# A two-matrix MLP in split fp32: which operand streams, how wide, and where the residual is added

## The chip, the cores and the metric

One core of a Trainium2 chip runs one program. The metric is the device time of one execution in microseconds (us); lower is better. The profile comes from one execution of its own, so its numbers are compared with that execution's time, and the median of the runs stands beside it. The engines are named as in the profile: PE is TensorE (matmuls), PEld its weight loads, DVE is VectorE, ACT is ScalarE, POOL is GpSimd, SP is SyncE, whose queue issues most DMAs.

## The reference

A decoder block on 256 tokens with a model width of 2048, in fp32. Two token mixers run ahead of the part that matters here, which is the end of the layer and the last normalization:

```python
h = x + gt1 * ((sig(gA) * y_A + sig(gB) * y_B) @ w_out)
u = rmsnorm(h, g_mlp) * (1 + sc2) + sh2
h = h + gt2 * (relu(u @ w_up) ** 2 @ w_down)      # w_up 2048 x 8192, w_down 8192 x 2048
out = rmsnorm(h, g_final)
```

`gt2` (like `sc2` and `sh2`) is a row of 2048 values, one sixth of `silu(c) @ w_ada + b_ada`.

## The kernel before

**Split fp32.** A product of two fp32 matrices is computed with three faster matmuls. Each operand is split into a rounded part `hi` (type fp32r) and a remainder `lo`; the product is hi x hi + hi x lo + lo x hi. For weights, `Unit.prep` makes `hi` with a ScalarE copy (helper `copy`, line 117) and `Unit.prep_lo` makes `lo` with a VectorE subtraction (helper `tt`, line 120). Both work on a raw tile of 128 x 1024 weights that the SP queue has loaded (line 210). There are 7 raw buffers, and 3 each of hi and lo.

**Units.** All work is a list of units, one raw tile each. `run_units` goes through the list: it issues the loads up to 7 units ahead, makes `hi` of unit i, issues the matmuls of unit i-2 (`SPLIT = 2`), then makes `lo` of unit i, then runs what was deferred to this index (`defer(n, fn)` runs `fn` n units later), then the steps of background generators that are due. Each engine works through its own instructions in the order in which they are issued there. A unit that only feeds VectorE (`gemm=False`, the adaLN products) has no hi or lo; `weave` spreads such units among others.

**A pass.** `gemm_pass` computes 1024 output columns. Weights are the loaded operand in blocks of 128x128, and the activations, in channel order (channels on the partitions, 256 tokens in the free dimension), stream as 256 columns. For each of 8 column blocks j, the unit issues three matmuls (lines 315, 317, 318). Two blocks share one PSUM bank, and the four banks A0 to A3 hold a pass. In the last unit of a pass, `finish(b, ps)` is called as soon as bank b is complete, and the next pass starts again with A0. `joint` is the number of units at the end of a pass whose matmuls are held and then issued block by block, so that the banks are completed one after the other.

**The MLP.** The first matrix (`up_units`) is 8 passes of 16 units over the normalized activations in region RU; `finish` is a ReLU out of PSUM into region RX (line 1415), and the square follows one unit later (line 1416). Among these units are woven 32 adaLN units, which sum the products of `w_ada` rows with `cond` for the two halves of `gt2` on VectorE (line 129). At the end of each half `fin1` sums over the partitions with matmuls (line 965) and `fin2` turns the result into columns with four transposes. The second matrix (`down_units`) is 2 passes of 64 units; `xprep` splits the hidden activations on the way (hi and lo of 128x256 per unit). `finish` there adds `gt2` times the result to the residual `hs["h"]`, which is in channel order, scales by `g_final`, squares, and `turn` transposes into token order with four PE transposes per bank (line 1466). The last batch also sums the squares over the channels with matmuls of one column (line 1359), and `last` scales by the reciprocal root and issues eight stores on the SP and ACT queues (line 1492).

**Another product of the same kernel.** `vs_units` computes the value projection the other way round: activations are the loaded operand, and 512 weight columns stream (lines 897 to 899).

Of the kernel before, what the change touches and what calls it, by code (L numbers as in the profile page):

```python
# [36 lines left out]
J_PROJ, J_GLU, J_OUT, J_UP, J_DOWN = 1, 1, (1, 2), 1, (1, 2)  # L37
# [44 lines left out]
def block_kernel(ctx, tc, cst_in, x, c, w_ada, b_ada, g_mix, w_in, w_ck2, pe_ck,  # L82
# [78 lines left out]
    small = cp.tile([128, 8], FT, name="small")  # L161

# [166 lines left out]

    BA = ["A0", "A1", "A2", "A3"]  # L330
# [139 lines left out]
    def rstd(o, ssum, t):  # L470

        A.activation(out=t, in_=ssum, func=AF.Sqrt)
# [511 lines left out]

    def ada2_pe_units(vec, quarter):
# [399 lines left out]
    def u2_start(row):  # L1385
        r = region("RU", 8192)
# [13 lines left out]
    class U2View:  # L1400
        def __init__(self, key):
            self.key = key

        def __getitem__(self, i):
            return u2[self.key][i]

    def up_units():
        res = []
        for g in range(8):
            def finish(b, ps, g=g):  # L1410
                if "h" not in h1:
                    h1["h"] = region("RX", 16384).rearrange("p (k t) -> p k t", k=64)
                ct = g * 8 + 2 * b
                o = h1["h"][:, ct:ct + 2, :].rearrange("p k t -> p (k t)")
                A.activation(out=o, in_=ps, func=AF.Relu)
                defer(1, lambda: A.activation(out=o, in_=o, func=AF.Square))
            res += gemm_pass(w_up[0], 1024 * g, list(range(16)), 1024, True, True, (U2View("h"), U2View("l")), BA, finish, joint=J_UP)
        return res

    fin = {}  # L1420

    def down_units():
        def slot(i):
# [6 lines left out]
        for g in range(2):  # L1430
            made = {}
# [8 lines left out]
            def finish(b, ps, g=g):  # L1440
                if "o" not in fin:
                    fin["u"] = region("RU", 8192)
                    fin["o"] = fin["u"][:, 0:4096].rearrange("p (t n) -> p t n", t=2)
                    fin["acc"] = fin["u"][:, 4096:4608]
                    fin["sq"] = fin["u"][:, 4608:6656]
                    fin["t"] = region("RB1", 4096)
                ct = g * 8 + 2 * b
                h = hs["h"][:, ct:ct + 2, :]
                for j in range(2):
                    stt(h[:, j, :], ps[:, 256 * j:256 * j + 256], gt2_c[:, ct + j:ct + j + 1], h[:, j, :],  # L1450
                        OP.mult, OP.add)
                hv = h.rearrange("p k t -> p (k t)")
                acc = fin["acc"]
                t = fin["t"][:, 512 * b:512 * b + 512]
                for j in range(2):
                    if g == 0 or j == 0:
                        A.activation(out=t[:, 256 * j:256 * j + 256], in_=h[:, j, :], func=AF.Copy,
                                     scale=gfin_c[:, ct + j:ct + j + 1])
                    else:
                        ts(t[:, 256 * j:256 * j + 256], h[:, j, :], gfin_c[:, ct + j:ct + j + 1], OP.mult)  # L1460

                def turn():
                    pb = bank(("T0", "T3")[b % 2])
                    for tok in range(2):
                        for j in range(2):
                            PE.transpose(pb[:, tok * 256 + j * 128:tok * 256 + j * 128 + 128],
                                         t[:, 256 * j + 128 * tok:256 * j + 128 * tok + 128], ident)
# [150 lines left out]
```

## Time and profile before

| | |
|---|---|
| median of 3 runs | 1780.44 us (1776.47 to 1782.63) |
| time of the profiled execution | 1776.92 us |
| its span | 1775.1 us |
| mean granted TensorE clock | 0.989 |
| PE busy | 1718.9 us, 97% of the span, 15710 matmuls |
| PEld busy | 1620.6 us, 91%, 15710 weight loads |
| DVE busy | 1108.5 us, 62% |
| ACT busy | 856.3 us, 48% |
| DMA moved | 406.26 MB, 229 GB/s on average |
| loads of the two matrices | 128 each, 512 KB each |

How to read it: the duration of a matmul in the trace is from its start to its modelled end, and matmuls overlap, so the distance between starts is what one costs; a group's busy time counts overlaps once. "Idle before" is the time in which an engine had nothing running ahead of an instruction, with what released it. A line number can be that of a helper that many places call.

### The profile page before, as it was taken

How to read it: one execution, taken by the hardware profiler on the slowest of the kernel's cores; microseconds unless marked ns; L12 is line 12 of the kernel's file. 1: busy time of each engine (PE TensorE's matmuls, PEld its weight loads, DVE VectorE, ACT ScalarE, POOL GpSimd, SP SyncE). 2: the span in 40 equal slices, each digit the busy share in tenths (PEclk: the TensorE clock that was granted, in tenths of full speed). 3: DMA queues.
4: the chain of work that ended last, by engine and by line, in shares of the span. 5: the costliest groups of instructions: out<-in, count | busy, mean ns of one | idle time of the engine just before them, and what ended most of it. 6: DMA issues, size and time to landing. Idle time of an engine off the chain costs nothing.

```text
span 1775.1 us, 37647 instructions
## 1 busy us (share of the span) xinstructions
PE 1718.9 (97%) x15710; PEld 1620.6 (91%) x15710; DVE 1108.5 (62%) x2032; ACT 856.3 (48%) x1379; POOL 29.4 (2%) x51
## 2 busy tenths in 40 slices
PE   6999999999999999999999999999999999999997
PEld 4788898789999988888899999999999999999997
DVE  4868468347888966666656575555555555565554
ACT  3433443754333477655544454444444544464444
POOL 1000000300000000000000000000000000000000
PEclk8999999999999999999999999999999999999998
DMA  9988756858888867876667567777777565556662
GB/s 349 327 275 315 260 180 206 267 160 296 274 274 283 254 211 243 296 244 211 214 198 262 176 219 235 235 227 224 240 234 227 179 183 184 181 176 184 184 181 81
DMA packets 121802, 406.26 MB, mean 229 GB/s; under 512 B 13904, under 2 KB 18480, under 8 KB 120864
## 3 DMA queue, kind: packets, MB, share of 16 engines
q1 hardware_dynamic: 114480, 385.49, 67.1%
q10 hardware_dynamic: 5408, 9.75, 1.5%
q0 software_dynamic: 1744, 8.62, 1.4%
q8 instruction: 123, 2.02, 0.4%
q14 instruction: 47, 0.39, 0.1%
HBM read 384.84 MB, written 16.88 MB: 226 GB/s over the span
## 4 chain that ended last, share of the span: by engine, by line
PE 87%; DVE 5%; ACT 4%; DMA 2%; issue 1%; ACTq 0%; SPq 0%; DVEq 0%
PE A L315 25%; PE A L317 24%; PE A L318 24%; PE T L998 2%; DVE lo L120 2%; PE T L343 2%; ACT hi L117 1%; ACT RX L117 1%; DMA raw<-in_l_ada_dram 1%; PE T L809 1%; PE A L897 1%; DMA raw<-in_l_vals_dram 1%; PE A L899 1%; PE A L898 1%; PE T L737 0%
## 5 line engine op out<-in xcount | busy, mean ns | idle before, releaser
L120 DVE TENSOR_TENSOR lo<-raw,hi 128x1024 fp32r<-128x1024 f32 (+1 forms) x497 | 607.0, 1223 | 507.8 <-ACT hi L117 504.0
L117 ACT ACTIVATE hi<-raw 128x1024 fp32r<-128x1024 f32 (+1 forms) x497 | 523.1, 1055 | 580.5 <-PE A L317 539.0
L315 PE MATMUL A<-RU,hi 128*128 128x256 f32 x2560 | 740.2, 289 | 3.3 <-ACT hi L117 1.5
L318 PE MATMUL A<-RU,lo 128*128 128x256 f32 x2560 | 728.0, 284 | 1.5 <-DVE lo L120 1.5
L317 PE MATMUL A<-RU,hi 128*128 128x256 f32 x2560 | 727.8, 284 | 0.0
L315 PEld LDWEIGHTS A<-RU,hi 128*128 128x128 f32 x2560 | 494.3, 193 | 27.7 <-issue 20.9
L318 PEld LDWEIGHTS A<-RU,lo 128*128 128x128 f32 x2560 | 494.4, 193 | 2.0 <-DVE lo L120 1.9
L317 PEld LDWEIGHTS A<-RU,hi 128*128 128x128 f32 x2560 | 494.7, 193 | 0.3 <-DVE RU L129 0.2
L315 PE MATMUL A<-RB,hi 128*128 128x256 f32 x1280 | 363.9, 284 | 1.4 <-ACT RB L117 1.2
L317 PE MATMUL A<-RB,hi 128*128 128x256 f32 x1280 | 362.6, 283 | 0.2
L318 PE MATMUL A<-RB,lo 128*128 128x256 f32 x1280 | 362.2, 283 | 0.0
L315 PEld LDWEIGHTS A<-RB,hi 128*128 128x128 f32 x1280 | 245.7, 192 | 3.4 <-ACT RB L117 1.6
L317 PEld LDWEIGHTS A<-RB,hi 128*128 128x128 f32 x1280 | 245.7, 192 | 0.6 <-DVE RB L129 0.5
L318 PEld LDWEIGHTS A<-RB,lo 128*128 128x128 f32 x1280 | 245.6, 192 | 0.0
L117 ACT ACTIVATE RB<-RX 128x256 fp32r<-128x256 f32 x160 | 64.3, 403 | 27.4 <-DVE RX L129 27.4
L120 DVE TENSOR_TENSOR RX<-A,RX 128x512 f32<-128x512 f32 x60 | 40.4, 687 | 30.2 <-PE A L318 29.2
L129 DVE SCALAR_TENSOR_TENSOR s<-raw,cond,s 128x1024 f32<-128x1024 f32 x45 | 57.6, 1279 | 0.1
L117 ACT ACTIVATE RX<-T 128x256 f32<-128x256 f32 (+2 forms) x81 | 39.8, 638 | 35.8 <-PE T L1204 26.6
L120 DVE TENSOR_TENSOR RB<-RX,RB 128x256 fp32r<-128x256 f32 x128 | 53.4, 418 | 1.6 <-ACT RB L117 1.6
L343 PE MATMUL T<-raw,cond 128*32 128x256 f32 x512 | 40.8, 413 | 10.0 <-DMA raw<-in_l_ada_dram 10.0
L998 PE MATMUL T<-raw,cond 128*32 128x128 f32 x1280 | 43.2, 276 | 2.0 <-ACT RX L117 2.0
L998 PEld LDWEIGHTS T<-raw,cond 128*32 128x32 f32 x1280 | 32.5, 109 | 8.4 <-ACT RX L117 4.2
(237 smaller groups left out, 1248.1 us busy)
## 6 DMA issues: line engine op xcount, KB each, us to landing
raw<-in_l_ada_dram SPq DMA_DIRECT2D x144, 512.0 KB, 4.9
raw<-in_w_in_dram SPq DMA_DIRECT2D x144, 512.0 KB, 4.6
raw<-in_w_up_dram SPq DMA_DIRECT2D x128, 512.0 KB, 4.2
raw<-in_w_down_dram SPq DMA_DIRECT2D x128, 512.0 KB, 4.5
raw<-in_w_ada_dram SPq DMA_DIRECT2D x48, 512.0 KB, 4.1
raw<-in_w_glu_dram SPq DMA_DIRECT2D x32, 512.0 KB, 5.1
raw<-in_w_out_dram SPq DMA_DIRECT2D x32, 512.0 KB, 5.8
raw<-in_l_keys_dram SPq DMA_DIRECT2D x16, 512.0 KB, 4.4
```

Source lines behind the costliest of these rows:

```text
L117: A.activation(out=out, in_=in_, func=AF.Copy, scale=scale)
L120: V.tensor_tensor(out=out, in0=a, in1=b, op=op)
L129: V.scalar_tensor_tensor(out=out, in0=a, scalar=s, in1=b, op0=op0, op1=op1)
L315: PE.matmul(out=o, lhsT=w.hi[:, at], rhs=xh, start=first and j % 2 == 0, stop=False, skip_group_check=True)
L317: PE.matmul(out=o, lhsT=w.hi[:, at], rhs=xl, start=False, stop=False, skip_group_check=True)
L318: PE.matmul(out=o, lhsT=w.lo[:, at], rhs=xh, start=False, stop=last, skip_group_check=True)
L343: PE.matmul(out=ps[q:q + 32, :], lhsT=cond[:, t0 + t:t0 + t + 1].to_broadcast([128, 32]), rhs=r[:, t, :], start=t0 == 0, stop=t0 == 12, ti ...
L809: PE.matmul(out=ps[h][:, (w * 2 + r_) * 128:(w * 2 + r_) * 128 + 128], lhsT=bl[c4 // 2][64 * h:64 * h + 64, (gw + w) % 16, r_, :], rhs=stk ...
L897: PE.matmul(out=o, lhsT=xh, rhs=u.hi[:, at], start=kt == 0, stop=False)
L898: PE.matmul(out=o, lhsT=xl, rhs=u.hi[:, at], start=False, stop=False)
L899: PE.matmul(out=o, lhsT=xh, rhs=lo[:, at], start=False, stop=kt == 15)
L998: PE.matmul(out=ps[q:q + 32, 0:128], lhsT=cond[:, kt:kt + 1].to_broadcast([128, 32]), rhs=r[:, kt % 8, :], start=kt < 4, stop=kt >= 12, ti ...
```

## The change

* First matrix: pass 0 (1024 columns) stays as it was, now with its own `finish` called `first`. The remaining 7168 columns become 14 passes of 512 columns in `wide_pass`. A unit holds two k blocks of 128 rows with 512 columns each, loaded as two runs of 512 values per partition. For each of 4 column blocks and both k blocks there are two matmuls: `hi` against 512 columns, which are the hi and the lo activations side by side (a view with two pieces of 256), and `lo` against the 256 hi activations. A bank now holds one column block, with the lo activations' share in its upper half. `finish` copies that half on ScalarE, adds the lower half on VectorE, and one unit later VectorE computes max(v, 0) * v.
* Second matrix: the activations become the loaded operand (two token halves t), and 512 weight columns stream (two halves s_ of the 1024). There are 12 matmuls per unit, and the result is in token order. In pass 1 the last 3 units are held, where it was 2.
* `gt2` is made as a row on all partitions instead of columns: `row_units` replaces `ada2_units(3, ...)`, with four matmuls against a full block of ones, and the bias row and `g_final` are broadcast by two DMAs on POOL's queue.
* The residual is transposed into token order by a background generator, `h_tokens`, in eight steps during pass 0 of the second matrix.
* The finish works in token order: products with the rows, sums of squares through `accum_out`, the mean and root per token half, and eight stores, all on the SP queue. For columns 0 to 1023 the product with `g_final` is deferred work in pass 1.

```diff
-J_PROJ, J_GLU, J_OUT, J_UP, J_DOWN = 1, 1, (1, 2), 1, (1, 2)
+J_PROJ, J_GLU, J_OUT, J_UP, J_DOWN = 1, 1, (1, 2), 1, (1, 3)
...
+    def wide_pass(src, col0, pairs, finish):
+        made, res = {}, []
+
+        def run(u, k0):
+            if k0 == 0:
+                made["b"] = [bank(t) for t in BA]
+            for j in range(4):
+                o = made["b"][j]
+                for t in range(2):
+                    xp = pairs(k0 + t)
+                    at = slice(512 * t + 128 * j, 512 * t + 128 * j + 128)
+                    PE.matmul(out=o, lhsT=u.hi[:, at], rhs=xp, start=k0 + t == 0, stop=False, skip_group_check=True)
+                    PE.matmul(out=o[:, 0:256], lhsT=u.lo[:, at], rhs=xp[:, 0], start=False, stop=k0 + t == 15,
+                              skip_group_check=True)
+                if k0 == 14:
+                    finish(j, o)
+
+        for k0 in range(0, 16, 2):
+            v = src[k0 * 128:(k0 + 2) * 128, col0:col0 + 512].rearrange("(k p) n -> p k n", p=128)
+            res.append(Unit([(lambda r: r.rearrange("p (k n) -> p k n", k=2), v)], lambda u, k=k0: run(u, k)))
+        return res
...
+    def row_units():
+        def place():
+            r = region("RB1", 4096)
+            rows["g"], rows["f"] = r[:, 0:2048], r[:, 2048:4096]
+            nc.gpsimd.dma_start(out=rows["g"], in_=b_ada[:, A_GT2:A_GT2 + D].to_broadcast([128, D]))
+            nc.gpsimd.dma_start(out=rows["f"], in_=g_final.rearrange("(o n) -> o n", o=1).to_broadcast([128, D]))
...
+            def fin_(i):
+                ps = bank("T3")
+                PE.matmul(out=ps, lhsT=ones, rhs=hold["a"][:, 512 * i:512 * i + 512], start=True, stop=True)
+                o = rows["g"][:, 1024 * half + 512 * i:1024 * half + 512 * i + 512]
+                tt(o, ps, o, OP.add)
+                if i == 0:
+                    defer(FIN_GAP, lambda: fin_(1))
...
     def up_units():
...
+        def pairs(kt):
+            return fr(u2["r"]).rearrange("p (s k t) -> p k s t", s=2, k=16)[:, kt]
...
+        res += gemm_pass(w_up[0], 0, list(range(16)), 1024, True, True, (Part("h"), Part("l")), BA, first, joint=J_UP)
+        for g in range(2, 16):
             def finish(b, ps, g=g):
...
+                if b % 2 == 0:
+                    h1["st"] = stage()
+                st = h1["st"][:, 256 * (b % 2):256 * (b % 2) + 256]
+                copy(st, ps[:, 256:512])
+                tt(st, ps[:, 0:256], st, OP.add)
+                if b % 2:
+                    st = h1["st"]
+                    ct = g * 4 + b - 1
+                    o = h1["h"][:, ct:ct + 2, :].rearrange("p k t -> p (k t)")
+                    defer(1, lambda: stt(o, st, 0.0, st, OP.max, OP.mult))
+            res += wide_pass(w_up[0], 512 * g, pairs, finish)
...
+    def h_tokens():
+
+        fin["u"] = region("RU", 8192)
+        fin["h"] = fin["u"][:, 0:4096].rearrange("p (t n) -> p t n", t=2)
+        fin["m"] = fin["u"][:, 4096:6144]
+        for i in range(8):
+            t, q = i // 4, i % 4
+            ps = bank(("T0", "T3")[i % 2])
+            for j in range(4):
+                PE.transpose(ps[:, 128 * j:128 * j + 128], hs["h"][:, 4 * q + j, 128 * t:128 * t + 128], ident)
+            copy(fin["h"][:, t, 512 * q:512 * q + 512], ps)
+            yield
...
+            def finish(t, c, ps):
+                h = fin["h"][:, t, 512 * c:512 * c + 512]
+                cs = slice(512 * c, 512 * c + 512)
+                m = fin["m"][:, 512 * (2 * t + c % 2):512 * (2 * t + c % 2) + 512]
+                if c < 2:
...
+                    defer(10 + 2 * t + c, lambda: tt(h, h, rows["f"][:, cs], OP.mult))
+                    return
+                tt(m, ps, rows["g"][:, cs], OP.mult)
+                tt(h, m, h, OP.add)
+                A.activation(out=m, in_=h, func=AF.Square, accum_out=ssq[:, 4 * t + c:4 * t + c + 1])
+                if (t, c) == (1, 2):
+                    mean(0)
+                if (t, c) == (1, 3):
+                    roots(0)
+                    mean(1)
+                    store(0, 3)
+                    roots(1)
+                    store(0, 0)
+                    store(1, 3)
...
+            def store(t, q):
+                r_ = small[:, 2 + t:3 + t]
+                v = fin["h"][:, t, 512 * q:512 * q + 512]
+                if q >= 2:
+                    stt(v, v, r_, rows["f"][:, 512 * q:512 * q + 512], OP.mult, OP.mult)
                 else:
...
+                    A.activation(out=v, in_=v, func=AF.Copy, scale=r_)
+                nc.sync.dma_start(out=out[0, t * 128:t * 128 + 128, 512 * q:512 * q + 512], in_=v)
+
+            def run(u, kt, g=g, held=held, acc=acc, finish=finish):
+                if kt == 0:
+                    acc["b"] = [bank(t) for t in BA]
+                held.append((u, kt))
+                if kt != 63 and 64 - kt <= J_DOWN[g]:
+                    return
+                for t in range(2):
+                    for s_ in range(2):
+                        o = acc["b"][2 * t + s_]
+                        at_ = slice(512 * s_, 512 * s_ + 512)
+                        for w, k in held:
+                            xh, xl = (x_[:, 128 * t:128 * t + 128] for x_ in w.xs)
+                            PE.matmul(out=o, lhsT=xh, rhs=w.hi[:, at_], start=k == 0, stop=False)
+                            PE.matmul(out=o, lhsT=xl, rhs=w.hi[:, at_], start=False, stop=False)
+                            PE.matmul(out=o, lhsT=xh, rhs=w.lo[:, at_], start=False, stop=k == 63)
+                        if kt == 63:
+                            finish(t, 2 * g + s_, o)
+                held.clear()
...
-        units += up[:UP_WAIT] + weave(up[UP_WAIT:], [u for h in range(2) for u in ada2_units(3, h, "T3")])
+        units += up[:UP_WAIT] + weave(up[UP_WAIT:], row_units())
...
+            dict(name="ht", gen=h_tokens(), start=marks["down"] + 6, end=marks["down"] + 46, total=8),
```

## Rows read from the trace of the kernel before

**Rows 1.** Page, part 4: the chain that ended last, share of the span by engine.
```profile
PE 87%; DVE 5%; ACT 4%; DMA 2%; issue 1%; ACTq 0%; SPq 0%; DVEq 0%
```

**Rows 2.** Windows in the first and second matrix: busy us (instructions), PEclk, DMA share, GB/s.
```profile
1020.00:1380.00 360.00, 360.00 (x2985) 357.66 (x2985) 200.07 (x184) 166.35 (x195) 0.00 (x0) 1.00 0.72 229
1400.00:1752.00 352.00, 352.00 (x2937) 352.00 (x2936) 195.03 (x255) 172.94 (x260) 0.00 (x0) 1.00 0.58 176
```

**Rows 3.** TensorE's waits, 985 to 1765 us: total us, times, longest us.
```profile
PE A L315 <- ACT RU L386: 1.5, 1, 1.5
PE T L1378 <- DVE small L129: 1.3, 1, 1.3
```

**Rows 4.** Timeline, second matrix: start us, us, engine, line, op, shapes, [idle before].
```profile
1700.64 0.28 PE L315 MATMUL A<-RB,hi 128*128 128x256 f32 x1
...
1700.72 1.06 ACT L117 ACTIVATE hi<-raw 128x1024 fp32r<-128x1024 f32 x1 [1.52 <-PE A L317]
...
1701.81 1.22 DVE L120 TENSOR_TENSOR lo<-raw,hi 128x1024 fp32r<-128x1024 f32 x1 [1.32 <-ACT hi L117]
...
1703.52 0.28 PE L315 MATMUL A<-RB,hi 128*128 128x256 f32 x1
```

**Rows 5.** Timeline, TensorE, value projection: matmuls of 512 columns.
```profile
293.58 0.39 PE L898 MATMUL A<-hi,RU 128*128 128x512 f32 x1
...
298.57 0.39 PE L899 MATMUL A<-lo,RU 128*128 128x512 f32 x1
...
316.51 0.40 PE L898 MATMUL A<-hi,RU 128*128 128x512 f32 x1
...
318.83 0.39 PE L899 MATMUL A<-lo,RU 128*128 128x512 f32 x1
```

**Rows 6.** Timeline of the end; then the DMA share in 40 slices, 1766 to 1775.1 us.
```profile
1761.89 0.28 PE L318 MATMUL A<-RB,lo 128*128 128x256 f32 x1
...
1762.21 0.88 DVE L129 SCALAR_TENSOR_TENSOR RS<-A,ada,RS 128x256 f32<-128x256 f32 x2
...
1763.14 0.61 ACT L1351 ACTIVATE RU<-RS 128x512 f32<-128x512 f32 x1
...
1766.95 2.41 SPq L1492 DMA_DIRECT2D out_dram<-RU  x4
...
DMA  0000000189999999999999999999999930000000
```

**Rows 7.** Lines by shape, VectorE (busy us, mean ns); one ScalarE line of the timeline.
```profile
L120 DVE TENSOR_TENSOR lo<-raw,hi 128x1024 fp32r<-128x1024 f32 x496 | 606.1, 1224 | 502.0 <-ACT hi L117 498.2 <-DMA d_v<-st 2.5 <-DMA raw<-in_l_ada_dram 1.1
...
L120 DVE TENSOR_TENSOR RB<-RX,RB 128x256 fp32r<-128x256 f32 x128 | 53.4, 418 | 1.6 <-ACT RB L117 1.6
L120 DVE TENSOR_TENSOR RX<-A,RX 128x512 f32<-128x512 f32 x60 | 40.4, 687 | 30.2 <-PE A L318 29.2
...
1014.79 0.38 ACT L117 ACTIVATE rbc<-T 128x256 f32<-128x256 f32 x1 [1.77 <-PE T L1378]
```

**Rows 8.** Timeline, TensorE: sums over partitions, attention scores, and four transposes.
```profile
760.40 0.62 PE L1153 MATMUL T<-RX 128*128 128x272 f32 x2
760.86 0.62 PE L1154 MATMUL T<-RX 128*128 128x272 f32 x2
...
1371.62 0.28 PE L318 MATMUL A<-RU,lo 128*128 128x256 f32 x1
...
1373.03 0.28 PE L317 MATMUL A<-RU,hi 128*128 128x256 f32 x1
...
1577.83 0.28 PE L318 MATMUL A<-RB,lo 128*128 128x256 f32 x1
...
1578.51 0.28 PE L317 MATMUL A<-RB,hi 128*128 128x256 f32 x1
```

**Rows 9.** DMA, 840 to 868 us: queue, packets, MB, share; issues, KB, us to landing.
```profile
q1 hardware_dynamic: 2352, 5.77, 61.7%
...
raw<-in_w_glu_dram SPq DMA_DIRECT2D x7, 512.0 KB, 4.5
```

More of the change, by code (lines that the diff above doesn't have):

```diff
@@ L161, in block_kernel @@
     small = cp.tile([128, 8], FT, name="small")
+    ssq = cp.tile([128, 8], FT, name="ssq")
     ru = region("RU", 8192)
@@ L468, in keep_x, with rstd @@
         yield
-    def rstd(o, ssum, t):
-        A.activation(out=t, in_=ssum, func=AF.Sqrt)
+    def rstd(o, ssum, t, rooted=False):
+        if not rooted:
+            A.activation(out=t, in_=ssum, func=AF.Sqrt)
         V.reciprocal(out=o, in_=t)
@@ new lines, in up_units, with __init__, __getitem__, first @@
+        class Part:
+            def __init__(self, key):
+                self.key = key
+            def __getitem__(self, i):
+                return u2[self.key][i]
+        def first(b, ps):
+            if "h" not in h1:
+                h1["h"] = region("RX", 16384).rearrange("p (k t) -> p k t", k=64)
+            o = h1["h"][:, 2 * b:2 * b + 2, :].rearrange("p k t -> p (k t)")
+            A.activation(out=o, in_=ps, func=AF.Relu)
+            defer(1, lambda: A.activation(out=o, in_=o, func=AF.Square))
@@ L1430, in down_units @@
         for g in range(2):
-            made = {}
+            made, held, acc = {}, [], {}
             def xprep(kt, made=made):
@@ L1438, in xprep @@
                 return made[kt]
[L1440 to L1458, printed above, removed]
-                    else:
[L1460 to L1467, printed above, removed]
-                    o = fin["o"][:, :, ct * 128:ct * 128 + 256]
-                    copy(o, pb.rearrange("p (t n) -> p t n", t=2))
-                if g == 0:
-                    defer(1, lambda: sumsq(hv, acc, ct == 0))
-                    defer(1 + b, turn)
-                else:
-                    squares(b, hv, acc, fin["sq"][:, 512 * b:512 * b + 512], fin.pop("turn", None))
-                    fin["turn"] = turn
-                    if b == 3:
-                        turn()
-                        last()
@@ L1496, in weave @@
+            for kt in range(64):
+                u_ = Unit([(lambda r: r, w_down[0, kt * 128:(kt + 1) * 128, 1024 * g:1024 * g + 1024])],
+                          lambda u, k=kt, run=run: run(u, k), xprep=lambda k=kt, xprep=xprep: xprep(k))
+                u_.joint = J_DOWN[g] > 1 and kt == 63
+                res.append(u_)
+        return res
     def weave(main, extra, tail=6, head=0):
```

66 lines of the change are left out of this document (39 added, 27 removed).

## The prediction, made blind

> **What bounds the kernel now.** I read the chain of waits first: 87% of the chain that ended last is TensorE work, 5% VectorE, 4% ScalarE [rows 1]. Then the stretches of the two matrices that the change touches. In the first matrix's 360 us and in 352 us of the second's, TensorE is busy for the whole stretch at a granted clock of 1.00 (2.4 GHz), VectorE for 200 and 195 us, ScalarE for 166 and 173 us, and the DMA engines are at 0.72 and 0.58 [rows 2]. Last, what TensorE waited for from the end of the output projection to the end of the second matrix: two waits, 2.8 us together, both ahead of the first matrix [rows 3]. So in both matrices the time is the number of matmuls times the spacing of their starts; the reported 0.28 us of one overlaps the next ones and is no price. The spacing: the first matmul of one weight part starts at 1700.64, that of the next at 1703.52, with 24 matmuls of 256 columns in each, so 120.0 ns each [rows 4]. 256 columns at 2.4 GHz are 106.7 ns; 13.3 ns are something else, paid once per 256 columns.
>
> The same kernel shows matmuls of 512 columns, with the activations as the loaded operand and the weight columns streaming, which is what the second matrix will have. In the longest stretch without a pause, 22 starts lie between 293.58 and 298.57: 226.8 ns each [rows 5]. 512 columns are 213.3 ns, so the excess is 13.5 ns, the same as at 256 columns: it goes with the matmul, not with the column. In shorter stretches, ten after a stop, it is 232 ns (316.51 to 318.83) [rows 5].
>
> **The change, step by step.** *First matrix, 14 of 16 parts.* Before, a 128x128 block of weights meets three matmuls of 256 columns (hi with both activation parts, lo with one). After, it meets one of 512 and one of 256. There are 14 x 8 units x 8 blocks = 896 of each. One pair of 240.0 ns becomes 226.8: 896 x 13.2 ns = **-11.8 us**. No row has a 512-column operand made of two pieces of 256, nor 512 and 256 in turn. The bounds: it costs like two of 256 (240 ns, nothing gained), or the excess of the narrow matmul vanishes behind the wide one (another 896 x 13.3 = 11.9 us gained). I take the fixed excess, since both widths show it.
>
> *Second matrix.* 2 x 64 units had 24 matmuls of 256; they get 12 of 512. 3072 x 120.0 = 368.6 us become 1536 x 226.8 = 348.4: **-20.3 us**. With 232 ns it would be 356.4, so -12.3. I take 226.8 because the stages of the change run without stops, as that stretch did.
>
> The Trainium skill speaks against both: "TensorE: Matmul & The Clock Gate" (section "Back-to-back issue gap") gives a warm gap of columns/2.4 ns plus about 2.5 ns. By it a pair of 256 costs 218.4 and a 512 costs 215.8, the 2432 replacements would give 6.3 us instead of 32.1, and the sum below would be -6.0 us. Rows 4 and 5 disagree with it at both widths, by some 11 ns, in matmuls that each load new weights.
>
> *The new evictions of the first matrix.* They leave TensorE's path if they end in time. A unit lasts 8 x (226.8 + 120.0) = 2.77 us. Counted from the start of a pass's last unit, bank j is complete for its readers at 0.69 x (j + 1) + 0.20 us (a reader starts 0.32 us after the start of the bank's last matmul, 1761.89 to 1762.21 [rows 6], so 0.20 after its slot of 0.12). Then a ScalarE copy of 128x256 out of PSUM, 0.38, and a VectorE sum, 0.42 [rows 7]. Bank 0 is free at 1.7, needed at 2.8; bank 3 is free at 3.8, needed at 4.9. What is queued behind the waiting sum on VectorE is the lo part of the unit two ahead: 3.8 + 1.22 [rows 7] = 5.0, and its first matmul wants it at 2 x 2.77 + 0.23 = 5.8. So 0.75 us of cover, and I cost it at nothing; each us beyond it would cost 14 us (14 passes). Behind the waiting copy on ScalarE is the hi part of the unit three ahead, wanted some 3 us later. VectorE is busy for 200 of 360 us now [rows 2]; 56 sums of 0.42 and 28 squares of 0.69 [rows 7] add 43, which leaves room.
>
> *The gate row.* Before, per half of the last adaLN vector, TensorE gives up 1.17 us for the sums over partitions (the second matmul after 1371.62 starts at 1373.03 instead of 0.24 later) [rows 8] and, I take it, what four transposes cost below, 0.44: 3.2 us for both halves. After, four sums of 512 fp32 columns over a full 128x128 operand. Nearest: 272 fp32 columns take 0.46 us (760.40 to 760.86) [rows 8], so 0.87 for 512, and about 0.1 for the change of shape: 4.0 us. **+0.8 us** (between 0 and 2). The two row broadcasts on POOL's queue have nothing behind them and are wanted only after 16 woven products, some 60 units later.
>
> *The residual in token order.* 32 transposes as before, in eight groups of four. One group costs 0.44 us (second matmul after 1577.83 at 1578.51 instead of 1578.07) [rows 8]. Before, seven groups lie ahead of the last matmul and one behind it; after, all eight lie ahead: **+0.4 us**.
>
> *The last three units in one batch.* Three buffers for hi, so the hi part of the last unit can start only when the fourth unit from the end is done. hi starts 0.08 us after the next unit's first matmul, lo 1.09 us later and takes 1.22 (1700.64, 1700.72, 1701.81) [rows 4]: ready at 2.35 us, wanted by the ninth matmul at 8 x 0.227 = 1.81. With two held units, as before, that wait was covered by one more unit. **+0.5 us**.
>
> *The finish.* Before, the last matmul's slot ends at 1762.01, the first store is issued at 1766.95, and the span ends 8.15 us after that at 1775.1 [rows 6]. The stores keep the DMA engines at nine tenths for 23 of 40 slices of 0.23 us, some 5.3 us for 2.1 MB [rows 6]: they are limited by the transfer, so the first issue counts. After: reader's lag 0.20, product and sum 2 x 0.69 [rows 7], square 0.61 [rows 6], mean, variance and first product about 1.3 by the size of before's small steps (estimate): issue at 3.5 instead of 4.9 us. **-1.4 us** (between +1 and -3).
>
> Sum: -11.8 - 20.3 + 0.8 + 0.4 + 0.5 - 1.4 = -31.8 us. The profiled execution took 1776.9 us (span 1775.1), the median of the runs is 1780.4. I put the difference to the median: **1748.6 us**.
>
> **Rivals.** *A: the wide matmul is dearer.* All 2432 at 232 ns give back 12.6 us: 1761.2. Or the two-piece operand costs 240 in the first matrix: 11.8 back, 1760.4. For it: the only long steady stretch at 226.8 is one, eleven shorter ones are between 229 and 233. Against: those have a stop at their head.
> *B: the narrow matmul's excess hides behind the wide one* in the first matrix: 1748.6 - 11.9 = 1736.7. For it: the next weight load has 227 ns instead of 120. Against: after a wide matmul the excess is still 13.5 [rows 5].
> *C: no change.* The excess goes with columns in such streams, or with weight traffic, and a 512 costs 240 everywhere: 32.1 us go back, 1780.7. The rows of 512 speak against it.
> *D: slower, through the weight loads.* In the 14 wide parts a load reads runs of 2 KB instead of 4 KB. 360 us at 229 GB/s are 82.4 MB [rows 2]; 112 loads of 0.524 MB are 58.7 of these, 0.51 of the share of 0.72. If 2 KB runs cost twice per byte, the share is 1.23, that is 443 us of transfer in a stage in which TensorE needs 348: 83 us more than now, 20 us gained elsewhere, 1843. It decides from 1.49 times the cost per byte. Against: 840 to 868 us, where most of the moved bytes are 2 KB runs of the GLU weight, 5.77 MB take 61.7% of 28 us, 334 GB/s of busy engine, and such a load lands after 4.5 us [rows 9]; the stretch of 4 KB runs has 229/0.72 = 318. So 2 KB runs are no dearer.
>
> **How the numbers follow.** Forecast 0.64 (its own range 1741 to 1756, from the gate row, finish and pace); A 0.18; B 0.08; C 0.05; D 0.03; 0.02 for something unnamed. From 1738 to 1763 the range holds the forecast, A, and the nearer half of B; left out are C, D, the rest of B. Faster by over 0.3% (5.3 us, about what a measurement of this kernel can tell from none): forecast, A, B and half of the unnamed, 0.91. Same: C, 0.05. Slower: D and the other half, 0.04.
>
> **What would show it.** Right: starts 227 ns after a wide and 120 ns after a narrow matmul, 2.77 us per unit in the first matrix and 2.72 in the second; no wait of TensorE at the 14 pass ends; one wait of about 0.5 us for lo in the last batch; the first store about 3.5 us after the last matmul's slot; the two stages some 12 and 20 us shorter, and everything ahead of them unchanged. Wrong: 232 or 240 ns between wide starts; a wait for lo after each pass; waits of the hi copy for a weight load; a DMA share near 1 in the first matrix. If the two stages shrink by under 20 us together, the term of the fixed excess was mis-sized.

## The result, and the profile after

The changed kernel takes 1754.1 us (median of 4 runs, 1750.1 to 1755.8) against 1780.5 us before: ratio 0.9853, 95% interval 0.9832 to 0.9875, 26.4 us less. Forecast were 1748.6 us and 31.8 us less. The direction and most of the size are right; 5 us are missing. The experiments separate two main causes: a pair of matmuls that costs more than forecast, and waits that were not forecast.

The page after: span, busy time by engine, and the chain's shares, which answer to [rows 1].

```profile
span 1754.0 us, 32823 instructions
...
PE 1693.2 (97%) x13246; PEld 1490.6 (85%) x13246; DVE 1150.7 (66%) x2120; ACT 841.7 (48%) x1376; POOL 30.5 (2%) x53
...
PE 86%; DVE 5%; ACT 5%; DMA 2%; issue 1%; ACTq 0%; SPq 0%; DVEq 0%
```

There are 2464 matmuls fewer, and TensorE is still 97% busy and 86% of the chain. PEld fell from 91 to 85%: a wide matmul leaves time in which no weight load runs.

The windows of the kernel before, cut at three points of each trace: the first matmul of the first matrix, the first of the second matrix, and the end of the last matmul's slot. Columns as in [rows 2].

```profile
1016.29:1390.75 374.46, 374.46 (x3088) 371.88 (x3089) 208.55 (x195) 174.50 (x207) 0.00 (x0) 0.99 0.71 225
1390.75:1762.01 371.26, 371.26 (x3098) 371.22 (x3097) 206.35 (x274) 185.16 (x282) 0.00 (x0) 1.00 0.56 171
1762.01:1775.10 13.09, 4.02 (x34) 3.62 (x32) 3.91 (x13) 5.44 (x10) 0.00 (x0) 0.62 0.44 160
```

The same three windows after:

```profile
1019.59:1386.67 367.08, 367.08 (x2185) 323.88 (x2185) 244.53 (x277) 165.31 (x209) 0.00 (x0) 0.99 0.71 229
1386.67:1742.10 355.43, 353.22 (x1570) 290.84 (x1568) 211.14 (x277) 181.47 (x276) 0.00 (x0) 1.00 0.54 178
1742.10:1754.00 11.90, 0.16 (x1) 0.00 (x0) 5.53 (x16) 3.80 (x10) 0.00 (x0) 0.73 0.50 176
```

The first matrix is 7.4 us shorter (374.46 to 367.08), the second 15.8 (371.26 to 355.43), the finish 1.2 (13.09 to 11.90): 24.4 us together. All that lies ahead is the same code, yet the first matmul of the first matrix starts at 1016.3 in one profile and at 1019.6 in the other. So the spans differ by 21.1 us only (1775.1 to 1754.0). In the other profiles shown below that start lies anywhere from 1013.6 to 1020.3 us, whatever the edit, so this is the runs' own spread. That is why the stages are compared here, and the medians for the total. The DMA share in the first matrix is 0.71 in both windows: the loads in runs of 2 KB cost no more, and they land after 4.0 us.

What TensorE waited for after, from 980 to 1760 us, answering to [rows 3]:

```profile
PE A L316 <- ACT RU L411: 1.5, 1, 1.5
PE A L1603 <- DVE lo L120: 1.4, 3, 0.5
PE T L1440 <- DVE small L129: 1.3, 1, 1.3
PE A L1601 <- ACT hi L117: 0.8, 1, 0.8
```

The first and third row are the old ones. There is no wait at the ends of the 14 passes: the new evictions stay under their cover. The other two are in the second matrix: 1.4 us for `lo`, 0.8 us for `hi`. One of the four times is the last batch, as forecast. The other three are not in the prediction.

The new matmuls of the first matrix, an excerpt in the middle of a pass (PE lines, start first):

```profile
1099.95 0.40 PE L344 MATMUL A<-RU,hi 128*128 128x512 f32 x1
1100.19 0.28 PE L345 MATMUL A<-RU,lo 128*128 128x256 f32 x1
1100.31 0.40 PE L344 MATMUL A<-RU,hi 128*128 128x512 f32 x1
...
1101.37 0.40 PE L344 MATMUL A<-RU,hi 128*128 128x512 f32 x1
```

From 1099.95 to 1101.37 are four pairs, so 355 ns here. Over the whole stretch, leaving out the four places where a sum for the gate row comes between, the trace's starts in ns give 235.4 ns from a wide to the narrow one behind it and 116.7 from there to the next wide: 352.1 ns for a pair, where 226.8 + 120.0 = 346.8 was forecast. (The expectations below have 234.7 and 117.3, from starts rounded to 10 ns as the timeline prints them; the sum is the same.) The second matrix, in a stretch without a stop:

```profile
1582.27 0.39 PE L1601 MATMUL A<-hi,RB 128*128 128x512 f32 x1
...
1584.99 0.39 PE L1601 MATMUL A<-hi,RB 128*128 128x512 f32 x1
```

12 matmuls in 2.72 us: 226.7 ns, the forecast.

Where the unforeseen waits are: VectorE, ScalarE and one restarted matmul (of the three between 1586 and 1593 us) early in the second matrix's second pass, with the idle time before each and its releaser.

```profile
1582.76 0.42 DVE L120 TENSOR_TENSOR RB<-RX,RB 128x256 fp32r<-128x256 f32 x1
...
1583.10 0.69 DVE L120 TENSOR_TENSOR RU<-RU,RB 128x512 f32<-128x512 f32 x1
...
1583.82 0.69 DVE L120 TENSOR_TENSOR RU<-RU 128x512 f32<-128x512 f32 x1
...
1584.54 0.63 ACT L1548 ACTIVATE RU<-RU 128x512 f32<-128x512 f32 x1 [2.66 <-DVE RU L120]
...
1585.08 0.19 ACT L1548 ACTIVATION_READ_ACCUMULATOR RU<-RU 128x1 f32 x1
1585.17 1.04 ACT L117 ACTIVATE hi<-raw 128x1024 fp32r<-128x1024 f32 x1
...
1586.25 1.23 DVE L120 TENSOR_TENSOR lo<-raw,hi 128x1024 fp32r<-128x1024 f32 x1 [1.74 <-ACT hi L117]
...
1587.53 0.50 PE L1603 MATMUL A<-lo,RB 128*128 128x512 f32 x1 [0.53 <-DVE lo L120]
...
1587.73 0.68 DVE L120 TENSOR_TENSOR RU<-RU,RB 128x512 f32<-128x512 f32 x1
```

One unit's deferred work is read here in order. On VectorE the product (1583.10) and the sum (1583.82) of the finish come behind the unit's own work. ScalarE's square (1584.54) has been waiting 2.66 us for the sum, with the `hi` copy of the next unit queued behind it; that starts at 1585.17. `lo` follows it at 1586.25, and TensorE gets it at 1587.53. The round goes over two engines one after the other and takes some 4.6 us, where a unit of TensorE takes 2.72. It comes four units in a row.

The end, answering to [rows 6]: the last batch's wait, the last matmul, the last square, the first store.

```profile
1735.62 0.50 PE L1603 MATMUL A<-lo,RB 128*128 128x512 f32 x1 [0.37 <-DVE lo L120]
...
1741.87 0.39 PE L1603 MATMUL A<-lo,RB 128*128 128x512 f32 x1
...
1743.75 0.63 ACT L1555 ACTIVATE RU<-RU 128x512 f32<-128x512 f32 x1 [1.22 <-DVE RU L120]
...
1745.53 0.82 SPq L1587 DMA_DIRECT2D out_dram<-RU  x2
```

The slot of the last matmul ends at 1742.10, and the first store is issued 3.43 us later (3.5 forecast). The span ends 8.5 us after that, where it was 8.15 before.

### The profile page after: what moved, and what is told of

It is laid out like the page before. It is cut to its first block, busy times and chain, and to the rows that moved or that the text cites. A ratio compares the mean times of both kernels' runs of the same rounds, so it can differ in the third digit from the quotient of the medians.

```text
span 1754.0 us, 32823 instructions
## 1 busy us (share of the span) xinstructions
PE 1693.2 (97%) x13246; PEld 1490.6 (85%) x13246; DVE 1150.7 (66%) x2120; ACT 841.7 (48%) x1376; POOL 30.5 (2%) x53
## 4 chain that ended last, share of the span: by engine, by line
PE 86%; DVE 5%; ACT 5%; DMA 2%; issue 1%; ACTq 0%; SPq 0%; DVEq 0%
PE A L316 12%; PE A L344 12%; PE A L318 12%; PE A L319 12%; PE A L1603 6%; PE A L1601 6%; PE A L1602 6%; PE A L345 6%; PE T L1060 2%; DVE lo L120 2%; PE T L368 1%; ACT hi L117 1%; ACT RX L117 1%; DMA raw<-in_l_ada_dram 1%; DMA raw<-in_l_vals_dram 1%
## 5 line engine op out<-in xcount | busy, mean ns | idle before, releaser
L316 PE MATMUL A<-RU,hi 128*128 128x256 f32 x1664 | 486.0, 292 | 3.3 <-ACT RU L411 1.5
L318 PE MATMUL A<-RU,hi 128*128 128x256 f32 x1664 | 474.2, 285 | 0.0
L316 PEld LDWEIGHTS A<-RU,hi 128*128 128x128 f32 x1664 | 322.4, 194 | 26.4 <-issue 20.1
L318 PEld LDWEIGHTS A<-RU,hi 128*128 128x128 f32 x1664 | 322.6, 194 | 0.3 <-DVE RU L129 0.2
L344 PE MATMUL A<-RU,hi 128*128 128x512 f32 x896 | 317.3, 399 | 0.0
L344 PEld LDWEIGHTS A<-RU,hi 128*128 128x128 f32 x896 | 168.2, 188 | 41.7 <-issue 0.7
L1603 PE MATMUL A<-lo,RB 128*128 128x512 f32 x512 | 199.7, 390 | 1.4 <-DVE lo L120 1.4
L1601 PE MATMUL A<-hi,RB 128*128 128x512 f32 x512 | 200.2, 391 | 0.8 <-ACT hi L117 0.8
L1602 PE MATMUL A<-hi,RB 128*128 128x512 f32 x512 | 199.2, 389 | 0.0
L1603 PEld LDWEIGHTS A<-lo,RB 128*128 128x128 f32 x512 | 96.1, 188 | 22.7 <-DVE lo L120 2.7
L1601 PEld LDWEIGHTS A<-hi,RB 128*128 128x128 f32 x512 | 96.1, 188 | 21.0 <-ACT hi L117 1.4
L1602 PEld LDWEIGHTS A<-hi,RB 128*128 128x128 f32 x512 | 96.1, 188 | 19.6
L316 PE MATMUL A<-RB,hi 128*128 128x256 f32 x256 | 73.6, 287 | 1.4 <-ACT RB L117 1.2
L318 PE MATMUL A<-RB,hi 128*128 128x256 f32 x256 | 72.7, 284 | 0.2
L319 PE MATMUL A<-RB,lo 128*128 128x256 f32 x256 | 72.3, 283 | 0.0
```

Of the source, the lines that this page charges most:

```text
L316: PE.matmul(out=o, lhsT=w.hi[:, at], rhs=xh, start=first and j % 2 == 0, stop=False, skip_group_check=True)
L318: PE.matmul(out=o, lhsT=w.hi[:, at], rhs=xl, start=False, stop=False, skip_group_check=True)
L319: PE.matmul(out=o, lhsT=w.lo[:, at], rhs=xh, start=False, stop=last, skip_group_check=True)
L344: PE.matmul(out=o, lhsT=u.hi[:, at], rhs=xp, start=k0 + t == 0, stop=False, skip_group_check=True)
L1601: PE.matmul(out=o, lhsT=xh, rhs=w.hi[:, at_], start=k == 0, stop=False)
L1602: PE.matmul(out=o, lhsT=xl, rhs=w.hi[:, at_], start=False, stop=False)
```

## The experiments

Each is the changed kernel with the edit shown. Stage times are from the traces, cut as above; "the stretch of the wide passes" is from their first matmul to the first of the second matrix, 318.87 us in the changed kernel.

### One run of 512 columns instead of two pieces

```diff
-                    PE.matmul(out=o[:, 0:256], lhsT=u.lo[:, at], rhs=xp[:, 0], start=False, stop=k0 + t == 15,
+                    PE.matmul(out=o[:, 0:256], lhsT=u.lo[:, at], rhs=xp[:, 0:256], start=False, stop=k0 + t == 15,
...
-        u2["h"] = fr(r[:, 0:4096]).rearrange("p (k t) -> p k t", k=16)
-        u2["l"] = fr(r[:, 4096:8192]).rearrange("p (k t) -> p k t", k=16)
+        v = fr(r).rearrange("p (k s t) -> p k s t", k=16, s=2)
+        u2["h"], u2["l"] = v[:, :, 0, :], v[:, :, 1, :]
...
-            return fr(u2["r"]).rearrange("p (s k t) -> p k s t", s=2, k=16)[:, kt]
+            return fr(u2["r"])[:, 512 * kt:512 * kt + 512]
```

> In the changed kernel a wide matmul of the first matrix and the narrow one behind it take 234.7 + 117.3 = 352.1 ns between starts, where 226.8 + 120.0 = 346.8 was predicted; over 896 pairs that is 4.7 us. Here the hi and lo activations of a k block lie side by side, so that the wide operand is one run of 512 columns. Theory P (the two pieces of the operand cost the 5.3 ns): the pair falls to 346.8 ns and the stretch of the 14 wide passes from 318.9 to about 314.1 us. Theory W (a change of width from one matmul to the next costs it): the pair stays at 352 ns and the stretch at 318.9 us.

```profile
1149.63 0.40 PE L344 MATMUL A<-RU,hi 128*128 128x512 f32 x1
...
1151.75 0.40 PE L344 MATMUL A<-RU,hi 128*128 128x512 f32 x1
```

Six pairs lie between these two starts, 353 ns each. Over the whole stretch it is 235.4 + 116.5 = 351.9 ns for a pair, and 318.73 us. The two pieces are not the cause; theory P falls.

### Wide, wide, narrow, narrow

```diff
-                for t in range(2):
-                    xp = pairs(k0 + t)
...
+                for t in range(2):
+                    at = slice(512 * t + 128 * j, 512 * t + 128 * j + 128)
+                    PE.matmul(out=o, lhsT=u.hi[:, at], rhs=pairs(k0 + t), start=k0 + t == 0, stop=False, skip_group_check=True)
+                for t in range(2):
+                    at = slice(512 * t + 128 * j, 512 * t + 128 * j + 128)
+                    PE.matmul(out=o[:, 0:256], lhsT=u.lo[:, at], rhs=pairs(k0 + t)[:, 0], start=False, stop=k0 + t == 15,
+                              skip_group_check=True)
```

> The order within a column block is wide, wide, narrow, narrow instead of wide, narrow, wide, narrow; operands and their number are as in the changed kernel, the wide one still in two pieces. Theory P (two pieces): four starts take 704.2 ns as before, the stretch of the wide passes stays at 318.9 us. Theory W (changes of width): half of the changes are left, so four starts take 693.6 + 5.3 = 698.9 ns and the stretch shrinks by 2.4 us to 316.5.

Its timeline, where equal neighbours are merged into one row (x2):

```profile
1149.69 0.63 PE L343 MATMUL A<-RU,hi 128*128 128x512 f32 x2
1150.15 0.40 PE L346 MATMUL A<-RU,lo 128*128 128x256 f32 x2
1150.38 0.63 PE L343 MATMUL A<-RU,hi 128*128 128x512 f32 x2
...
1152.47 0.62 PE L343 MATMUL A<-RU,hi 128*128 128x512 f32 x2
```

Four groups of wide and narrow lie between 1149.69 and 1152.47: 695 ns each. Over the whole stretch it is 696.7 on average, and the stretch is 315.52 us, 3.35 less than in the changed kernel. The same matmuls on the same operands, in another order: the direction is theory W's, and the gain is larger than its 2.4 us.

### The deferred finish work in every fourth unit

```diff
                         tt(h, m, h, OP.add)
+
+                    def square():
                         A.activation(out=m, in_=h, func=AF.Square, accum_out=ssq[:, 4 * t + c:4 * t + c + 1])
...
-                    defer(4 + 2 * t + c, rest)
-                    defer(10 + 2 * t + c, lambda: tt(h, h, rows["f"][:, cs], OP.mult))
+                    n = 4 + 4 * (2 * t + c)
+                    defer(n, rest)
+                    defer(n + 1, square)
+                    defer(n + 2, lambda: tt(h, h, rows["f"][:, cs], OP.mult))
```

> In the changed kernel TensorE waits three times between 1586 and 1593 us in the second pass of the second matrix, some 2.7 us with the slower restarts. Theory: the deferred work of the finish (four times a VectorE sum and, right behind it, a ScalarE square that waits for it, in four units in a row) holds back the hi copies behind the squares. Here this work falls in every fourth unit, and the square comes one unit after the sum. Expected: no wait there, the second matrix 2.5 to 2.7 us shorter (355.4 to about 352.8 us from its first matmul to the end of its last slot). Rival (the hi copies wait for raw tiles or free buffers at the change of pass, whatever is deferred): the waits stay, 355.4 us.

TensorE's waits in it, over the same 780 us as above:

```profile
PE A L316 <- ACT RU L411: 1.5, 1, 1.5
PE T L1440 <- DVE small L129: 1.3, 1, 1.3
PE A L1607 <- DVE lo L120: 0.4, 1, 0.4
```

Its second matrix, columns as above:

```profile
1383.66:1736.35 352.69, 352.32 (x1570) 291.23 (x1568) 211.27 (x277) 181.75 (x276) 0.00 (x0) 1.00 0.55 179
```

Only the last batch's 0.4 us are left of the waits in the second matrix, and that stage takes 352.69 us instead of 355.43: 2.7 us. Moving the deferred work ends the waits, with raw tiles and buffers as they were, so this work was the cause, and the rival falls. The edit does two things at once: the work falls in every fourth unit, and the square comes one unit after its sum. Which of the two is enough, no run separates.

### Wide matmuls alone

The product of the lo weights is left out in the 14 wide parts.

```diff
-                    PE.matmul(out=o, lhsT=u.hi[:, at], rhs=xp, start=k0 + t == 0, stop=False, skip_group_check=True)
-                    PE.matmul(out=o[:, 0:256], lhsT=u.lo[:, at], rhs=xp[:, 0], start=False, stop=k0 + t == 15,
-                              skip_group_check=True)
+                    PE.matmul(out=o, lhsT=u.hi[:, at], rhs=xp, start=k0 + t == 0, stop=k0 + t == 15, skip_group_check=True)
```

> The product of the lo weights with the hi activations is left out in the 14 wide parts, so only wide matmuls with the two-piece operand are left there. Theory P (two pieces cost 5.3 ns): 232.1 ns between starts inside a unit. Theory W (changes of width): 226.8 ns, as in the second matrix. Both: TensorE may wait between units, since a unit then lasts only 1.8 us, little more than the 1.65 us of VectorE's work for one; the distance of starts inside a unit is what counts.

The first row of its wide passes:

```profile
1064.25 14.70 PE L344 MATMUL A<-RU,hi 128*128 128x512 f32 x64
```

64 wide matmuls with the two-piece operand follow each other without a stop. From the first start to the last end it is 14.70 us; less the last one's 0.39 that is 63 distances of 227.1 ns. Theory P would have needed 232.

### All wide ones of a unit first

```diff
+            for js in ([0, 1, 2, 3],) if k0 != 14 else ([0], [1], [2], [3]):
+                for j in js:
+                    for t in range(2):
...
+                        PE.matmul(out=made["b"][j], lhsT=u.hi[:, at], rhs=pairs(k0 + t), start=k0 + t == 0, stop=False,
+                                  skip_group_check=True)
+                for j in js:
+                    for t in range(2):
...
+                        PE.matmul(out=made["b"][j][:, 0:256], lhsT=u.lo[:, at], rhs=pairs(k0 + t)[:, 0], start=False,
+                                  stop=k0 + t == 15, skip_group_check=True)
```

> All eight wide matmuls of a unit come first, then its eight narrow ones (in the last unit of a pass still per column block: wide, wide, narrow, narrow). Theory W (each change between the widths costs): the runs so far give 10.6 ns per four starts with four changes (the changed kernel) and about 3.1 ns with two (wide, wide, narrow, narrow), so 3 to 5 ns per pair of changes; here 154 pairs of changes are left of 896. Expected: 16 starts of a unit take about 2778 ns (2774 without any cost), and the stretch of the wide passes falls to 314.5 us, from 318.9 in the changed kernel and 315.5 with the grouping in fours. Rival (what the second order gained comes from something else in it, such as the lo weights being read later): no change against 315.5 us.

One unit and the start of the next, merged rows again:

```profile
1151.22 2.00 PE L343 MATMUL A<-RU,hi 128*128 128x512 f32 x8
1153.06 1.12 PE L348 MATMUL A<-RU,lo 128*128 128x256 f32 x8
1154.02 0.40 PE L343 MATMUL A<-RU,hi 128*128 128x512 f32 x1
```

Eight wide ones take 1.84 us (230 ns each) and eight narrow ones 0.96 (120 each): 2.80 us for the unit, and the stretch takes 316.18 us. That is 2.7 less than in the changed kernel, but not the 314.5 expected, and 0.7 more than with groups of two. So the cost is not proportional to the number of changes: theory W as I had put it is wrong in its size. Within the eight, each wide matmul is 3 ns dearer on average than in a long wide stream, and the trace's starts in ns show where. Averaged by place, the first five behind the narrow ones take 233.4, 235.7, 228.4, 232.5 and 230.8 ns, and the last three 226.7. Of the narrow ones the first takes 113.3 ns, the second 119.3, and the others 120.0. Over the stretch that makes 349.2 ns for a pair; the unit shown has 350.

### Groups of four

The same edit with `([0, 1], [2, 3])` in place of `([0, 1, 2, 3],)`.

> Groups of four wide and four narrow matmuls (two column blocks), between the groups of two (348.2 ns for a wide and a narrow one together) and of eight (350.0). If each of the first wide matmuls after a change is dearer (after a stop the second matrix shows 232 ns for the first six, then 228, then 227), the pair lies at 349 to 351 ns and the stretch at 316.0 to 316.8 us. If the number of changes decides, it lies below 348.2 ns and the stretch below 315.5 us.

```profile
1149.90 1.09 PE L343 MATMUL A<-RU,hi 128*128 128x512 f32 x4
1150.83 0.63 PE L348 MATMUL A<-RU,lo 128*128 128x256 f32 x4
1151.30 1.09 PE L343 MATMUL A<-RU,hi 128*128 128x512 f32 x4
1152.23 0.64 PE L348 MATMUL A<-RU,lo 128*128 128x256 f32 x4
1152.71 0.40 PE L343 MATMUL A<-RU,hi 128*128 128x512 f32 x1
```

Four wide ones take 0.93 us (232 to 233 ns each), four narrow ones 0.47 to 0.48 (118 to 120): 351 ns for a pair, and a stretch of 317.47 us, a little above the expected band. The number of changes does not decide. By place, over the stretch, the four wide ones take 234.2, 234.1, 232.4 and 228.5 ns and the narrow ones 117.4 to 119.1: as in the groups of eight, the first wide ones after a change are the dear ones.

### Every matmul 512 wide

```diff
-                    PE.matmul(out=o[:, 0:256], lhsT=u.lo[:, at], rhs=xp[:, 0], start=False, stop=k0 + t == 15,
+                    PE.matmul(out=o, lhsT=u.lo[:, at], rhs=xp, start=False, stop=k0 + t == 15,
                               skip_group_check=True)
```

> In the 14 wide parts the lo weights also meet all 512 columns (the product of lo weights and lo activations is added), so hi and lo weights still alternate into the same bank, but every matmul has 512 columns. Theory W (the change of width costs): 226.8 ns between starts, 453.6 for a pair, the stretch of the wide passes 112 x 16 x 226.8 ns + 3.4 = 409.8 us. Rival (it is the alternation of the hi and lo weights, or of the part of the bank that is written): above 230 ns as in the changed kernel, 415 to 420 us.

```profile
1149.90 0.39 PE L344 MATMUL A<-RU,hi 128*128 128x512 f32 x1
...
1152.16 0.39 PE L344 MATMUL A<-RU,hi 128*128 128x512 f32 x1
```

Ten matmuls in 2.26 us; over the whole stretch 226.9 ns from hi to lo and 226.6 from lo to hi, and 409.81 us. The alternation of hi and lo weights costs nothing. What costs comes with the two widths. A narrow matmul also writes only half of its bank, and no run separates that from its width; but in the kernel before, where the half changes after every third matmul and the width never does, the distance is 120.0 ns at that place too.

### The first matrix undone

```diff
-        res += gemm_pass(w_up[0], 0, list(range(16)), 1024, True, True, (Part("h"), Part("l")), BA, first, joint=J_UP)
-        for g in range(2, 16):
...
+        for g in range(8):
+            res += gemm_pass(w_up[0], 1024 * g, list(range(16)), 1024, True, True, (Part("h"), Part("l")), BA,
+                             lambda b, ps, g=g: first(b, ps, g), joint=J_UP)
```

> The first matrix is computed as before the change (16 parts in eight passes of 1024 columns, three matmuls of 256 per block, ReLU and square on ScalarE); everything else is as in the changed kernel. Theory: a pair of wide and narrow costs 352.1 ns where three narrow ones cost 360.0, so the 14 wide parts are worth 896 x 7.9 ns = 7.1 us, and this kernel is 7 to 8 us slower than the changed one and 19 us faster than the kernel before. Rival (the term as predicted, 13.2 ns for each, with the loss somewhere outside of this stage): 11.8 us slower than the changed one.

Its first matrix, columns as above:

```profile
1016.06:1390.61 374.55, 374.55 (x3080) 372.39 (x3081) 210.70 (x197) 173.53 (x205) 0.00 (x0) 0.99 0.71 225
```

374.55 us, as before the change (374.46), and 7.5 more than in the changed kernel. In time it is 1760.0 us, ratio 0.9898 [0.9883, 0.9913] to the kernel before, 7.7 us above the changed kernel run beside it (1752.3). The first part of the change is worth 7.5 us.

### The changed kernel again

No edit.

> The changed kernel once more, on the chip and between the runs of the two kernels above, so that their differences to it are measured beside it. Expected 1751 to 1756 us. The stretch ahead of the first matrix is the same code in every kernel here; in the profiled executions so far it took between 1014.9 and 1019.6 us. If that spread is the runs' own and nothing of the change, the first matrix starts between 1014 and 1020 us here too.

1752.3 us (1750.0 to 1752.8), ratio 0.9854 [0.9838, 0.9871]. Its first matrix starts at 1013.6 us, a little earlier than the range expected, which only widens the spread of the unchanged part; its two stages take 367.27 and 355.45 us.

### Three edits together, twice

The deferred work in every fourth unit, and the last batch of three held units in another order, with all wide matmuls of a unit first:

```diff
-                for t in range(2):
-                    for s_ in range(2):
+                every = list(range(len(held)))
+                if len(held) == 3:
+                    order = [(0, 0, [0, 1]), (0, 1, [0, 1]), (0, 0, [2]), (0, 1, [2]), (1, 0, every), (1, 1, every)]
+                else:
+                    order = [(t, s_, every) for t in range(2) for s_ in range(2)]
+                for t, s_, part_ in order:
```

> Three edits together: all wide matmuls of a unit ahead of its narrow ones; the deferred finish work in every fourth unit with the square one unit after its sum; and in the batch of the last three units the third unit's matmuls of the first bank come after the first two units' of the second bank. Theory: 4.4 us from the order, 2.7 us from the deferred work, 0.5 us from the last batch: 7.6 us less than the changed kernel, about 1746.5 against 1754.1, ratio 0.981 to the kernel before. No wait of TensorE in the second matrix. Rival (the waits come back somewhere else, or the freed time falls on the finish): under 4 us less.

1748.5 us (1747.6 to 1750.1), ratio 0.9833 [0.9818, 0.9847]. No wait is left in the second matrix, which takes 352.00 us, 3.4 less; the wide passes take 316.18, 2.7 less. That is 6.1 us in these two stretches, and 3.9 us in the medians, the changed kernel run beside it at 1752.3. By the medians alone this falls into the rival's range (under 4 us); by the trace no wait came back, and the finish is as long as it was, 11.92 us. Pass 0 of the first matrix, which no edit touches, took 49.2 us in this profile and 48.2 in the changed kernel's; the granted clock over its first 5 us was 0.50 and 0.57 (1.00 after them in the changed kernel, 0.98 here). The expected 4.4 us from the order were 2.7.

The same with wide, wide, narrow, narrow in its place:

> The order wide, wide, narrow, narrow in each column block (the stretch of the wide passes took 315.5 us with it), with the deferred finish work in every fourth unit and the reordered last batch (second matrix 352.0 us). Expected: the two stages as in the runs where each edit stood, 315.5 and 352.0 us, together 6.8 us below the changed kernel and 0.7 us below the version with all wide matmuls of a unit first (1748.5 us): about 1747.5 us. Rival (the edits do not add up): above 1750 us.

1746.5 us (1744.5 to 1749.9), ratio 0.9818 [0.9804, 0.9832]. Its windows, cut as above:

```profile
1020.32:1384.18 363.86, 363.86 (x2185) 321.96 (x2186) 243.78 (x277) 165.48 (x209) 0.00 (x0) 0.99 0.71 232
1384.18:1736.18 352.00, 352.00 (x1570) 291.30 (x1568) 211.17 (x277) 181.77 (x276) 0.00 (x0) 1.00 0.54 180
1736.18:1748.10 11.92, 0.16 (x1) 0.00 (x0) 5.53 (x16) 3.80 (x10) 0.00 (x0) 0.73 0.50 176
```

363.86, 352.00 and 11.92 us: against the changed kernel 3.2 and 3.4 us less in the two stages, and the same finish. The edits add up. This is the fastest version here. Its interval lies below that of the changed kernel's second set of runs (0.9838 to 0.9871) and meets that of the first at 0.9832; the 6.6 us in the two stages are read from the traces.

## Why the prediction was right, and where it was off

**What held.** The excess goes with the matmul: 226.8 ns in the second matrix, 240.0 for two narrow ones. That term was -20.3 us, and 1536 distances at 226.8 ns with eight groups of transposes (0.446 us each in the trace) are what the stage shows apart from the waits. The Trainium skill's gap of columns/2.4 ns plus 2.5 ("TensorE: Matmul & The Clock Gate", section "Back-to-back issue gap") is 11 ns below the trace here too, with new weights for each matmul; the page gives that gap for a single matmul by itself. Rival C (no change) is out, and so is D: the DMA share in the first matrix stayed at 0.71. The evictions stayed under their 0.75 us of cover in all 14 passes. The finish gave 1.2 us (1.4 forecast). The wait of the last batch came: 0.37 us idle, and 0.7 us in the stage with the slower restart (352.69 to 352.00 us when its order was changed), where 0.5 was forecast. A group of transposes costs the same as before.

**The term that was mis-sized.** First matrix, -11.8 us: it is -7.1, 896 times the 7.9 ns between 360.0 (three narrow ones) and 352.1. The step that failed is "I take the fixed excess, since both widths show it". Both rows were streams of one width; this one changes width at every matmul. The wide matmul is then 235.4 ns, not 226.8, and the narrow one 116.7, not 120.0. Neither the two pieces (351.9 ns without them) nor the alternation of weights (226.8 a matmul with one width) does it; the order of the same matmuls changes it (348.3 in groups of two). It lay inside the bounds given for this term. Rival A's first half has 232 ns for every wide matmul: for the pair of the first matrix that gives the right sum, for the second matrix it is wrong. I set the 232 ns of [rows 5] aside because those stretches "have a stop at their head", and the runs showed that narrow matmuls in between act much as a stop does: in groups of eight the first five wide ones behind them average 232 ns and the rest 226.7. That 232 + 120 gives the pair's 352 is luck, since the alternation shows 235.4 and 116.7.

**The term that was missing.** For the deferred work of the finish in the second pass of the second matrix the prediction has no term. It costs 2.7 us. The question that I asked of the copies and sums of the first matrix (what is queued behind the waiting instruction on its engine) was not asked of the square, which waits on ScalarE with a `hi` copy behind it.

**Small ones.** The gate row was put at +0.8 us and is about -0.1: a sum over 512 fp32 columns takes 0.86 us off the stream (1202.63 to 1203.84, less a pair), 3.4 for four; the two old sums (1.17 each) with their transposes (0.59 each, the second matmul after 1378.54 at 1379.37 in the trace before) cost 3.5.

The transposes were put at +0.4 us, by the reading that seven of the eight groups lay ahead of the last matmul before the change. That reading is wrong: the trace before has six ahead, and two that start after the last matmul, which starts at 1761.89 (timeline, TensorE):

```profile
1762.01 0.60 PE L1466 MATMUL T<-cst,RB 128*128 128x128 f32 x4
...
1765.04 0.99 PE L1466 MATMUL T<-cst,RB 128*128 128x128 f32 x4
```

So two groups were moved ahead, which is +0.9 us. And the `lo` of the last batch is ready at 2.39 us by its own rows (0.08 + 1.09 + 1.22), not at 2.35.

Together: -7.1 and -0.1 for the first matrix, where the stage shows -7.4. The 0.2 us left lie in pass 0, 48.4 us before and 48.2 after, whose first 5 us had a granted clock of 0.52 before and 0.57 after. The second matrix gives -15.8: -20.3, +0.9 for the transposes, +0.7 for the last batch, +2.7 for the wait, and 0.2 us are left over. With -1.2 for the finish that is 24.4 us, of 31.8 forecast. Of the gap of 7.4 us, 4.7 are the mis-sized pair and 2.7 the missing wait; the small ones (gate row -0.9; transposes +0.5, last batch +0.2, finish +0.2) cancel. The medians say 26.4, with an interval of 22 to 30 us, so both agree.

## What to carry to other kernels

Price a matmul by the distance of starts in a stream that looks like the new one; a row from a stream of one width does not hold where widths alternate. The first starts after a stop are a warning: here they were about as dear (232 ns) as the first wide ones after narrow ones. Where matmuls of two widths must mix, try the order: groups of two took 315.5 us where alternation took 318.9, at no other change. And for every deferred step ask what stands behind it on its engine while it waits, in particular where one step goes through two engines and several units in a row get it.

## What the runs showed that was not expected

A wide matmul's distance depends on what ran ahead of it. In a long stream of wide ones it is 226.8 ns; alternating with narrow ones 235.4; in groups of two 233; in groups of four 232 on average; in groups of eight 230, of which the first five carry all of the excess. After the transposes in the second matrix, the six distances behind the first restarted one are 232 ns on average in every other group, the next six 228, and then 227. The narrow one goes the other way: 120.0 in a stream, 116.7 alternating, 114.6 and 115.9 in groups of two, 113.3 for the first of eight. So a change to wide costs over several matmuls and a change to narrow gives a little back, and the groups are not ordered by the number of changes: groups of two are the cheapest mix (348.3 ns a pair), below eight (349.2), four (350.8) and one (352.1). Why that is so, and what in TensorE carries the memory over several matmuls, no run here shows; it stays open.
